# One scatter per expert into the output, and half of a plain float32 weight tile split in two

## The chip, the cores and the metric

One core of a Trainium2 chip runs the whole kernel. The metric is device microseconds for one execution, the median of several runs.

## The reference

A block of attention is followed by a mixture of experts, and the change lies in the second. The part that matters, cut:

```python
def hier_moe(u, wg, bg, we, be, w_gate, w_up, w_down):    # 2064 tokens, 64 experts in 8 groups
    g_p, g_idx = lax.top_k(g_prob, 1)                      # one group for each token
    e_p, e_idx = lax.top_k(jax.nn.softmax(e_logits, axis=-1), TOP_K)   # two experts of that group
    ...
    def expert_block(args):
        xb, e = args
        hdn = jax.nn.silu(xb @ w_gate[e]) * (xb @ w_up[e])   # 1024 -> 512
        return hdn @ w_down[e]                                # 512 -> 1024
    out = jnp.zeros((n_tok + 1, D), f32).at[slot_tok].add(ys.astype(f32) * slot_gate[:, None])[:n_tok]
...
    h = h + hier_moe(rmsnorm(h, ffn_norm[l]), ...)
return rmsnorm(h, final_norm)[:, N_META:]
```

Each token goes to two experts of one group. Its row of the result is the residual plus both experts' contributions, and then a norm over the row with the gains `final_norm`.

## The kernel before, in words

The kernel has an attention part (about the first 1200 us) and an expert part, `phase_moe`, which takes the rest. The expert part does one **turn** for each of the 64 experts, in an order that walks through the groups (the same group comes back every eight turns). An expert works on up to 112 token rows of 1024 numbers.

**Weights.** The three weight matrices of an expert come as six tiles of 128x2048 float32 numbers: g0 and g1 (gate), u0 and u1 (up), d0 and d1 (down). Five of them are split: ScalarE casts `raw` to a short float `hi`, VectorE subtracts, `lo = raw - hi`, and TensorE makes three cheap products in place of one (`mm3`: hi by hi, hi by lo, lo by hi). The sixth, d1, is multiplied as it is, in plain float32 (`down_whole`, rows `pd<-raw,hc`).

**A turn on TensorE**, always in this order: gate (M_g0, M_g1), turning the hidden rows of the expert before (TH), up (M_u0, M_u1), turning the next expert's rows (TX0, TX1), and down of the expert before (M_d0, M_d1a, M_d1).

**A turn on VectorE**, in the trace's names: `h` (the product with silu), `xl` twice (low parts of the token rows), `z` twice (the down result plus the row `b`), five `lo`, `o<-z,ss,gain` (the last norm), and `hl` (low parts of the hidden rows, without which M_d0 can't go past its second product).

**A turn on ScalarE**: five `hi`, `xh` twice, `sg` (silu), `o<-z` (squares, whose sum is `ss`), `hh` and `hc` (high parts and plain copy of the hidden rows).

**A turn on GpSimd**: `xs<-ud,src` gathers the token rows of a later expert; `b<-hz,src` gathers the rows of the array `hz` for the expert two turns on, into one of two buffers, so it has to wait for the second `z` of this turn; `hz<-z,t_zd` scatters `z` to `hz`; two small operations `ss` make the row's scale from the sum of squares (add EPS, power -0.5); `out_dram<-o,t_od` scatters the normed rows to the output. Both scatters are given all 112 rows. An index beyond 2047 makes a row be skipped: a token's first expert writes its row to `hz` alone, its second to the output alone (tables `t_zd` and `t_od`).

**Order.** `moe_plan` sets the order on TensorE, VectorE, ScalarE and GpSimd from a table of costs and due times, and `Ordered` keeps the compute instructions of an engine in it. Where the DMAs of GpSimd stand among them is settled when the program is built. Each engine works off its own queue in order: an instruction that waits holds up all behind it.

All expert instructions stand under the helper's line L124 in the profile (L123 after the change), so groups are told apart by their tiles.

Of the kernel before, what the change touches and what calls it, by code (L numbers as in the profile page):

```python
# [75 lines left out]
def build(tc, a, dbg=None, stop=99):  # L76
    nc = tc.nc
    dbg = dbg or {}
    with ExitStack() as top:
# [19 lines left out]
        nc.scalar.preload_act_table_set("natural_log_exp_and_others")  # L99
        env = dict(tc=tc, nc=nc, a=a, dbg=dbg, zf=zf, zv=zv, qd=qd, qrd=qrd, hg=hg, ud=ud, hz=hz, xlist=xlist, xexp=xexp,  # L100
                   ident=ident, ones=ones, eps=eps, out=a.get("out"))
        env["rt"] = {}
        with ExitStack() as ctx:
            env["ctx"] = ctx
            env["keep"] = ctx.enter_context(tc.tile_pool(name="keep", bufs=1))
            z_rest, z_close = phase_z(**env)
            env["right"] = right = ExitStack()
            kvp = right.enter_context(tc.tile_pool(name="kv", bufs=1, side=RIGHT))
            env["kv"] = ([kvp.tile([P, L], F32R, name=n) for n in ("ch", "cl", "kr_")]
                         + [kvp.tile([P, NT + 1, P], F32R, name=n) for n in ("vh", "vl")])  # L110
# [646 lines left out]

def phase_mix(tc, nc, a, qd, qrd, hg, ud, hz, xlist, xexp, kv, ident, ones, eps, rt, keep, ctx, right, g_rest, g_close, **_):
    ch, cl, kr_, vh, vl = kv
# [10 lines left out]
    with ExitStack() as out:  # L770
# [354 lines left out]
        def out_proj(i, xs, yh, yl, hs, t, hf):  # L1125
# [11 lines left out]
            if hf and hs[-1] == 3:  # L1137
                nc.sync.dma_start(hz[j * P:j * P + P], x)
# [277 lines left out]
def targets(nc, sp, rt):  # L1416
# [3 lines left out]
    first = first.rearrange("s g j -> s (g j)")  # L1420
    zd = rt["zd"] = sp.tile([BS, NE], I32, name="t_zd", bufs=1)
    od = rt["od"] = sp.tile([BS, NE], I32, name="t_od", bufs=1)
    nc.vector.scalar_tensor_tensor(od, first, float(FAR), rt["src"], op0=OP.mult, op1=OP.add)
    nc.vector.tensor_scalar(first, first, -float(FAR), float(FAR), op0=OP.mult, op1=OP.add)
    nc.vector.tensor_add(zd, first, rt["src"])


def moe_plan():
# [9 lines left out]
    for i, t in enumerate(TILES):  # L1438
        b, k = -(t[0] == "d"), i - HB
        old = ("M_" + TILES[k % n], -(k // n))  # L1440
        op("hi_" + t, b, "A", 1.95, old)
        op("lo_" + t, b, "V", 2.4, ("hi_" + t, 0), old)

# [3 lines left out]
    def cost(t):  # L1447
        return W if t in TILES else W * 4 / 3

# [92 lines left out]
    line.sort(key=lambda x: x[0])  # L1542
    return [(n, e, e + ops[n][0], nodes[n, e][0]) for _, (n, e) in line if n not in ("GD", "BQ", "ZQ", "OQ")]


def phase_moe(tc, nc, a, ctx, ud, hz, xlist, xexp, ident, ones, eps, rt, out, **_):
    rp = rt["rp"]
# [47 lines left out]
    def turn(S):  # L1595
        S.hn = 2 if NATIVE and S.e is not None else 4
        S.hh = sp.tile([P, 4, BS], F32R, name="hh", tag="hh", bufs=2)
# [11 lines left out]
    def hcopy(S):  # L1609
        S.hc = sp.tile([P, 2, BS], F32, name="hc", tag="hc", bufs=2)  # L1610
        on.scalar.copy(S.hc, S.ph[:, 2:])

    def down_whole(S, raw, hf):
        cs = slice(512 * hf, 512 * hf + 512)
        for k in range(2):
            on.tensor.matmul(S.d[hf], S.hc[:, k], raw[:, k, cs], start=False, stop=k == 1)

# [7 lines left out]
    rows = Block()  # L1625
    rows.put, rows.got, rows.sent = [], [], []

# [29 lines left out]

    def root(ss):
        on.gpsimd.tensor_scalar(ss, ss, EPS, None, op0=OP.add)
        on.gpsimd.tensor_tensor(ss, ss, half[:ss.shape[0]], op=OP.pow)  # L1660

    def last_norm(S):
        on.vector.scalar_tensor_tensor(S.o, S.z, S.ss, rows.gain[:BS], op0=OP.mult, op1=OP.mult)

    def leave(S):
        o = spread(out, rt["od"][:, S.e:S.e + 1], S.o)
        for q in rows.sent:
            tc.declare_no_dep(o.ins, q.ins, reason="rows of other tokens")
        rows.sent.append(o)

# [16 lines left out]
    def hi(S, t, eng):  # L1687
        load(S, t)
        if t == "d0" and NATIVE:
            load(S, "d1")  # L1690
        made[S.e, t].high(rp, eng)
# [7 lines left out]
    def mm_d(S, j, hf):  # L1699
        if f"d{j}" in NATIVE:  # L1700
            w = made[S.e, f"d{j}"] if hf == 0 else made.pop((S.e, f"d{j}"))
            return down_whole(S, w.view(w.raw), hf)
        w = made[S.e, f"d{j}"].parts() if hf == 0 else use(S, f"d{j}")
# [39 lines left out]
    with tc.For_i(0, again, 1):  # L1743
        nx = nc.values_load(nxi[0:1, 0:1], min_val=0, max_val=NX)
        with tc.For_i(0, nx, 1) as x:
# [34 lines left out]
            S.b = sp.tile([BS, D], F32, name="b", tag="b", bufs=BB)  # L1780
            gather(S.b, S.src, hz)
            for j in range(2):
# [16 lines left out]
            for hf in range(2):  # L1799
                plus(S, hf)  # L1800
            spread(hz, S.src, S.z)
        ft = sp.tile([P, NT, 8], F32, name="xft", tag="xft", bufs=1)
# [8 lines left out]
        for t in range(NT):  # L1811
            y = sp.tile([P, D], F32, name="xy", tag="z", bufs=ZB)
            nc.vector.memset(y, 0.0)
            gather(y, ix[:, t:t + 1], hz)
# [3 lines left out]
            root(ss)  # L1818
            nc.vector.scalar_tensor_tensor(o, y, ss, gain, op0=OP.mult, op1=OP.mult)
# [60 lines left out]
```

## Time and profile before

| what | value |
|---|---|
| median of 3 runs | 2450.58 us (2449.58 to 2459.94) |
| the profiled execution's own time | 2446.82 us |
| its span, first to last instruction | 2445.1 us |
| TensorE busy | 2350.4 us, 96% of the span |
| VectorE, ScalarE, GpSimd busy | 72%, 53%, 37% of the span |

The profiled execution took 1.72 us more than its span. Busy shares are averages over two parts with different limits; the expert part runs from about 1248 us to the end.

### The profile page before, as it was taken

The numbers are of one execution on the slowest core, as the hardware profiler recorded it, in microseconds if no ns is written. First come the engines' busy times: TensorE is split into PE (matmuls) and PEld (weight loads), VectorE is DVE, ScalarE is ACT, GpSimd is POOL, SyncE is SP. The second block draws the span as 40 slices with busy tenths as digits, with TensorE's granted clock in tenths as the row PEclk, the third lists the DMA queues.
The fourth block names the chain that finished last, engine by engine and source line by source line (L and its number), as shares of the span: only waits on it lengthen the run. The fifth ranks groups of instructions, "written<-read, shape, count | busy, mean of one in ns | idle before, by whom it ended". The sixth has DMA issues, their size and how long they took to land. (4 is left out here: it accounts for less than half of the span.)

```text
span 2445.1 us, 35600 instructions
## 1 busy us (share of the span) xinstructions
PE 2350.4 (96%) x12897; PEld 1870.6 (77%) x12897; DVE 1755.0 (72%) x2756; ACT 1303.9 (53%) x2018; POOL 905.4 (37%) x740
## 2 busy tenths in 40 slices
PE   7999999899999999999699999999999999999997
PEld 7899997677789989989566777676666666666664
DVE  6334334777567777767678888888888888888885
ACT  4211103555365555555366666666666666666663
POOL 0000002621000212111335556566656666666653
PEclk9999999899999999999899999999999999999999
DMA  6211115555331212111599999999999999999994
GB/s 210 76 62 66 65 43 158 167 164 178 130 109 61 79 61 82 55 68 44 218 326 389 380 386 376 386 375 381 369 367 367 375 370 381 369 366 375 374 359 182
DMA packets 161154, 571.70 MB, mean 234 GB/s; under 512 B 37132, under 2 KB 79644, under 8 KB 111820
## 3 DMA queue, kind: packets, MB, share of 16 engines
q1 hardware_dynamic: 125612, 509.71, 56.6%
q0 software_dynamic: 32912, 50.94, 6.5%
q10 hardware_dynamic: 2448, 8.72, 1.2%
q8 instruction: 103, 1.69, 0.3%
q14 instruction: 79, 0.65, 0.1%
HBM read 529.71 MB, written 106.63 MB: 260 GB/s over the span
## 5 line engine op out<-in xcount | busy, mean ns | idle before, releaser
L124 DVE TENSOR_TENSOR lo<-raw,hi 128x2048 fp32r<-128x2048 f32 x317 | 720.7, 2285 | 15.1 <-ACT hi L124 10.2
L124 ACT CAST hi<-raw 128x2048 fp32r<-128x2048 f32 x318 | 609.5, 1917 | 200.8 <-PE pg L124 132.7
L124 PE MATMUL pg<-hi,xh 128*112 128x512 f32 x1024 | 434.5, 424 | 0.0
L124 PE MATMUL pg<-hi,xl 128*112 128x512 f32 x1024 | 407.6, 398 | 2.7 <-DVE xl L124 2.7
L124 PE MATMUL pg<-lo,xh 128*112 128x512 f32 x1024 | 401.9, 392 | 0.0
L124 POOL DMA_INDIRECT hz<-z,t_zd x64 | 262.0, 4094 | 323.2 <-DVE z L124 314.5
L124 PEld LDWEIGHTS pg<-lo,xh 128*112 128x112 f32 x1024 | 180.5, 176 | 70.0 <-issue 7.1
L124 POOL DMA_INDIRECT out_dram<-o,t_od x64 | 193.6, 3025 | 105.0 <-DVE hl L124 82.4
L124 PEld LDWEIGHTS pg<-hi,xh 128*112 128x112 f32 x1024 | 179.3, 175 | 66.4 <-ACT xh L124 10.3
L124 PE MATMUL pd<-raw,hc 128*112 128x512 f32 x512 | 230.0, 592 | 0.0
L124 PEld LDWEIGHTS pg<-hi,xl 128*112 128x112 f32 x1024 | 178.9, 175 | 61.8 <-DVE xl L124 3.3
L135 PE MATMUL ps<-uh,wh 128*128 128x256 f32 (+3 forms) x768 | 218.7, 285 | 1.3 <-ACT uh L231 0.9
L136 PE MATMUL ps<-ul,wh 128*128 128x256 f32 (+3 forms) x768 | 218.3, 284 | 0.6 <-DVE ul L232 0.6
L137 PE MATMUL ps<-uh,wl 128*128 128x256 f32 (+3 forms) x768 | 217.4, 283 | 0.0
L124 DVE SCALAR_TENSOR_TENSOR o<-z,ss,gain 112x1024 f32<-112x1024 f32 x64 | 82.2, 1285 | 173.0 <-POOL ss L124 167.4
L124 PEld LDWEIGHTS pd<-raw,hc 128*112 128x112 f32 x512 | 90.1, 176 | 104.2 <-issue 97.0
L135 PEld LDWEIGHTS ps<-uh,wh 128*128 128x128 f32 (+1 forms) x768 | 144.7, 189 | 2.3 <-ACT uh L231 1.1
L136 PEld LDWEIGHTS ps<-ul,wh 128*128 128x128 f32 (+1 forms) x768 | 144.7, 188 | 1.5 <-DVE ul L232 0.8
L137 PEld LDWEIGHTS ps<-uh,wl 128*128 128x128 f32 (+1 forms) x768 | 144.7, 188 | 0.1
L124 POOL DMA_INDIRECT xs<-ud,src x64 | 126.6, 1978 | 40.7 <-issue 18.7
L338 POOL TENSOR_SCALAR_AFFINE_SELECT mf<-ones 128x128 f32<-128x128 f32 x2 | 0.6, 300 | 380.8 <-PE ps L137 380.8
L257 DVE COPY st<-ps 128x256 f32<-128x256 f32 (+1 forms) x64 | 26.9, 422 | 143.6 <-PE ps L137 143.6
(2413 smaller groups left out, 5302.8 us busy)
## 6 DMA issues: line engine op xcount, KB each, us to landing
raw<-in_w_gate_dram SPq DMA_DIRECT2D x128, 1024.0 KB
raw<-in_w_up_dram SPq DMA_DIRECT2D x128, 1024.0 KB
raw<-in_w_down_dram SPq DMA_DIRECT2D x128, 1024.0 KB
x<-in_x_dram SPq DMA_DIRECT2D x32, 512.0 KB
zf<-st SPq DMA_DIRECT2D x85, 128.0 KB
hg<-x SPq DMA_DIRECT2D x16, 512.0 KB
x<-hg SPq DMA_DIRECT2D x16, 512.0 KB
hz<-x SPq DMA_DIRECT2D x16, 512.0 KB
```

The costliest lines, as they stand in the source:

```text
L124: return self.tc.keep_in_program_order(f(*args, **kw))
L135: nc.tensor.matmul(out, lh, rh, start=start, stop=False, **kw)
L136: nc.tensor.matmul(out, lh, rl, start=False, stop=False, **kw)
L137: nc.tensor.matmul(out, ll, rh, start=False, stop=stop, **kw)
L257: nc.vector.tensor_copy(st[:w, :n - o], ps[:w, :n - o])
L338: nc.gpsimd.affine_select(mf[:, :, hh], ob, pattern=[[CH, 2], [1, CH]], compare_op=OP.is_ge, fill=0.0, base=0, channel_multiplier=-1)
```

## The change

1. The array `hz` goes. The residual is written to the output array itself, the rows `b` are gathered from there, and each expert scatters once, to the output: `out_dram<-o,src`, with all its tokens' rows.
2. What a row needs is chosen by numbers in place of indices. For a token's first expert the exponent of `ss` is 0 (table `t_hx`) and the gains are 1; for its second they are -0.5 and `final_norm`. ScalarE forms the matrix of gains for each expert (`GM`, an operation over 112x1024 numbers, `g<-gain,t_first,t_sec`), and the last norm reads `g` where it read `gain`.
3. Of the tile d1, the first 1024 of 2048 columns are split in hi and lo and multiplied by `mm3`; the other 1024 stay plain float32. So there is a sixth `hi` and a sixth `lo` in a turn, both of half width; `hl` and `hh` take 336 columns in place of 224, `hc` 112 in place of 224.
4. The planner's table follows: the scatter to `hz` (SZ) is out, GM is in, due times are moved.

```diff
-NATIVE = ("d1",)
-TILES = tuple(t for t in ("g0", "g1", "u0", "u1", "d0", "d1") if t not in NATIVE)
+TILES = ("g0", "g1", "u0", "u1", "d0", "d1")
+SPLIT = 1
...
-            eng.copy(self.hi, self.raw)
+            eng.copy(self.hi[:, :self.n], self.raw[:, :self.n])
...
-            eng.tensor_sub(self.lo, self.raw, self.hi.bitcast(F32))
+            eng.tensor_sub(self.lo[:, :self.n], self.raw[:, :self.n], self.hi[:, :self.n].bitcast(F32))
...
-    od = rt["od"] = sp.tile([BS, NE], I32, name="t_od", bufs=1)
-    nc.vector.scalar_tensor_tensor(od, first, float(FAR), rt["src"], op0=OP.mult, op1=OP.add)
...
+    sec = rt["sec"] = sp.tile([BS, NE], F32, name="t_sec", bufs=1)
+    nc.vector.tensor_scalar(sec, first, -1.0, 1.0, op0=OP.mult, op1=OP.add)
+    rt["fst"] = first
+    hx = rt["hx"] = sp.tile([BS, NE], F32, name="t_hx", bufs=1)
+    nc.vector.tensor_scalar_mul(hx, sec, -0.5)
...
-    op("GB", -1, "G", 1.7, ("Y1", BB), ("ZQ", 8))
+    op("GB", -1, "G", 1.7, ("Y1", BB), ("OQ", 8))
     op("BQ", -1, "Q", 5.0, ("GB", 0))
-    op("SZ", -1, "G", 2.1, ("Y1", 0))
-    op("ZQ", -1, "Q", 5.0, ("SZ", 0))
     op("SQ", -1, "A", 1.3, ("Y1", 0), ("OQ", OB))
-    op("RT", -1, "G", 0.3, ("SQ", 0))
-    op("L", -1, "V", 1.3, ("RT", 0))
+    op("RT", -1, "G", 1.3, ("SQ", 0))
+    op("GM", -1, "A", 1.1, ("L", 2))
+    op("L", -1, "V", 1.3, ("RT", 0), ("GM", 0))
...
-        for n, d in (("SZ", 2.5), ("SQ", 6.0), ("L", 9.0), ("SO", 10.0)):
+        for n, d in (("SQ", 3.0), ("L", 7.0), ("SO", 8.5)):
...
+        for k in range(SPLIT):
+            mm3(on, S.d[hf], S.hh[:, 2 + k], S.hl[:, 2 + k], hi[:, k, cs], lo[:, k, cs], False, False)
+        for k in range(SPLIT, 2):
+            on.tensor.matmul(S.d[hf], S.hc[:, k - SPLIT], raw[:, k, cs], start=False, stop=k == 1)
...
-        o = gather(S.b, S.src, hz)
+        o = gather(S.b, S.src, out)
...
+    def blend(S):
+        S.g = sp.tile([BS, D], F32, name="g", tag="g", bufs=2)
+        on.scalar.activation(S.g, rows.gain[:BS], AF.Identity, scale=rt["sec"][:, S.e:S.e + 1], bias=rt["fst"][:, S.e:S.e + 1])
...
-        on.vector.scalar_tensor_tensor(S.o, S.z, S.ss, rows.gain[:BS], op0=OP.mult, op1=OP.mult)
+        on.vector.scalar_tensor_tensor(S.o, S.z, S.ss, S.g, op0=OP.mult, op1=OP.mult)
...
-        o = spread(out, rt["od"][:, S.e:S.e + 1], S.o)
+        o = spread(out, S.src, S.o)
```

GpSimd, a turn in the middle of the expert part before the change, from one scatter to the output to the two `ss` operations, all turns alike:

```order
L124 DMA out_dram<-o,t_od 2048x1024
L124 DMA xs_13720<-ud,src 112x1024
L124 DMA hz<-z,t_zd 2048x1024
L124 DMA b<-hz,src 112x1024
L124 TENSOR_SCALAR ss<-ss 112x1
L124 TENSOR_TENSOR ss<-ss,half 112x1
```

GpSimd with the change, such a turn in the form that most have:

```order
L123 DMA out_dram<-o,src 2048x1024
L123 DMA b<-out_dram,src 112x1024
L123 DMA xs_13719<-ud,src 112x1024
L123 TENSOR_SCALAR ss<-ss 112x1
L123 TENSOR_TENSOR ss<-ss,t_hx 112x1
```

The scatter to `hz` is gone, and the gather `xs`, which stood ahead of it, now stands between the gather `b` and the two `ss`. That is so in 42 of the 64 turns (in two of these between the two `ss`); in the others `xs` stands ahead of `b` or behind the `ss`, so that `b` alone stands there, and in the last two neither does.

VectorE, the end of a turn and the start of the next before the change, around the last norm `o`:

```order
L124 TENSOR_TENSOR z<-pd,b 112x512
L124 TENSOR_TENSOR lo_19832<-raw,hi 128x2048
L124 TENSOR_TENSOR lo_19847<-raw,hi 128x2048
L124 SCALAR_TENSOR_TENSOR o<-z,ss,gain 112x1024
L124 TENSOR_TENSOR hl<-pth,hh 128x224
L124 TENSOR_TENSOR lo_19739<-raw,hi 128x2048
L124 TENSOR_TENSOR lo_19773<-raw,hi 128x2048
```

VectorE with the change, the same place:

```order
L123 TENSOR_TENSOR z<-pd,b 112x512
L123 TENSOR_TENSOR lo_19960<-raw,hi 128x2048
L123 TENSOR_TENSOR lo_19974<-raw,hi 128x2048
L123 SCALAR_TENSOR_TENSOR o<-z,ss,g 112x1024
L123 TENSOR_TENSOR hl<-pth,hh 128x336
L123 TENSOR_TENSOR lo_20015<-raw,hi 128x1024
L123 TENSOR_TENSOR lo_20033<-raw,hi 128x2048
L123 SCALAR_TENSOR_TENSOR h<-pg,grs,sg 112x128x4
L123 TENSOR_TENSOR xl<-pt,xh 128x448
L123 TENSOR_TENSOR lo_20055<-raw,hi 128x2048
```

The last norm still stands behind two `lo` of full width, and `hl` right behind the norm. The half-width `lo` of d1 is new, `hl` is wider, and one of the two `lo` that stood ahead of `h` has moved behind `xl`.

## Rows read from the trace of the kernel before

**Rows 1.** The page's first part: busy time, share, instructions by engine.

```profile
PE 2350.4 (96%) x12897; PEld 1870.6 (77%) x12897; DVE 1755.0 (72%) x2756; ACT 1303.9 (53%) x2018; POOL 905.4 (37%) x740
```

**Rows 2.** Busy time by stretch: stretch, length, busy (instructions) by engine, clock, DMA share, GB/s.

```profile
1230.00:1240.00 10.00, 8.74 (x33) 6.47 (x34) 7.27 (x14) 3.37 (x4) 0.58 (x1) 0.83 1.02 369
...
2100.00:2200.00 100.00, 99.06 (x424) 68.81 (x423) 84.12 (x64) 64.96 (x64) 61.12 (x31) 1.00 0.98 368
```

**Rows 3.** Timeline of TensorE, starts of plain products of d1: start, length, what.

```profile
1248.37 3.59 PE L124 MATMUL pd<-raw,hc 128*112 128x512 f32 x8
...
1619.90 3.59 PE L124 MATMUL pd<-raw,hc 128*112 128x512 f32 x8
...
1675.90 3.59 PE L124 MATMUL pd<-raw,hc 128*112 128x512 f32 x8
...
2400.54 3.59 PE L124 MATMUL pd<-raw,hc 128*112 128x512 f32 x8
```

**Rows 4.** Timeline of TensorE: plain and split products, and a wait in brackets.

```profile
1452.72 3.59 PE L124 MATMUL pd<-raw,hc 128*112 128x512 f32 x8
...
1456.39 0.39 PE L124 MATMUL pg<-lo,xh 128*112 128x512 f32 x1
...
1461.48 0.39 PE L124 MATMUL pg<-hi,xl 128*112 128x512 f32 x1
...
2054.84 0.49 PE L124 MATMUL pd<-hi,hl 128*112 128x512 f32 x1 [0.19 <-DVE hl L124]
```

**Rows 5.** Timeline, a turn of 19.07 us: VectorE, GpSimd and ScalarE around the last norm.

```profile
1641.85 0.61 DVE L124 TENSOR_TENSOR xl<-pt,xh 128x448 fp32r<-128x448 f32 x1
1642.38 2.28 DVE L124 TENSOR_TENSOR lo<-raw,hi 128x2048 fp32r<-128x2048 f32 x1
1644.58 0.68 DVE L124 TENSOR_TENSOR z<-pd,b 112x512 f32<-112x512 f32 x1
1645.18 4.48 DVE L124 TENSOR_TENSOR lo<-raw,hi 128x2048 fp32r<-128x2048 f32 x2
1645.54 4.96 POOL L124 DMA_INDIRECT hz<-z,t_zd  x1 [4.77 <-DVE z L124]
1646.81 1.05 ACT L124 ACTIVATE o<-z 112x1024 f32<-112x1024 f32 x1
1650.81 0.99 POOL L124 DMA_INDIRECT b<-hz,src  x1 [0.30 <-issue]
1652.80 1.29 DVE L124 SCALAR_TENSOR_TENSOR o<-z,ss,gain 112x1024 f32<-112x1024 f32 x1 [3.14 <-POOL ss L124]
1654.01 0.38 DVE L124 TENSOR_TENSOR hl<-pth,hh 128x224 fp32r<-128x224 f32 x1
1654.31 4.60 DVE L124 TENSOR_TENSOR lo<-raw,hi 128x2048 fp32r<-128x2048 f32 x2
```

**Rows 6.** Timeline, a turn of 18.58 us: VectorE and GpSimd ahead of the last norm.

```profile
1570.40 2.76 POOL L124 DMA_INDIRECT hz<-z,t_zd  x1 [5.27 <-DVE z L124]
1572.53 2.29 DVE L124 TENSOR_TENSOR lo<-raw,hi 128x2048 fp32r<-128x2048 f32 x1 [0.21 <-ACT hi L124]
1573.46 2.23 POOL L124 DMA_INDIRECT b<-hz,src  x1 [0.30 <-issue]
1576.70 1.28 DVE L124 SCALAR_TENSOR_TENSOR o<-z,ss,gain 112x1024 f32<-112x1024 f32 x1 [1.87 <-POOL ss L124]
```

**Rows 7.** Groups by line from 1660 to 2380 us: count, busy, mean ns, idle before.

```profile
L124 DVE SCALAR_TENSOR_TENSOR o<-z,ss,gain 112x1024 f32<-112x1024 f32 x38 | 48.8, 1285 | 119.7 <-POOL ss L124 119.7
...
L124 POOL DMA_INDIRECT hz<-z,t_zd x38 | 188.8, 4968 | 183.5 <-DVE z L124 183.5
```

**Rows 8.** Timeline of GpSimd near the end, where VectorE stands still.

```profile
2425.53 0.95 POOL L124 DMA_INDIRECT hz<-z,t_zd  x1 [5.21 <-DVE z L124]
```

**Rows 9.** Waits from 1300 to 2300 us: who waited for whom, total, times, longest.

```profile
ACT hc L124 <- DVE hl L124: 163.5, 52, 4.9
...
ACT hi L124 <- PE pg L124: 104.7, 49, 3.7
```

More of the change, by code (lines that the diff above doesn't have):

```diff
@@ L1440, in moe_plan @@
         old = ("M_" + TILES[k % n], -(k // n))
-        op("hi_" + t, b, "A", 1.95, old)
-        op("lo_" + t, b, "V", 2.4, ("hi_" + t, 0), old)
+        op("hi_" + t, b, "A", 1.05 if t == "d1" else 1.95, old)
+        op("lo_" + t, b, "V", 1.2 if t == "d1" else 2.4, ("hi_" + t, 0), old)
     def ready(t):
@@ L1447, in cost @@
     def cost(t):
-        return W if t in TILES else W * 4 / 3
+        return W * 7 / 6 if t == "d1" else W
     for i, t in enumerate(("g0", "g1", "u0", "u1")):
@@ L1542, in moe_plan, with phase_moe @@
     line.sort(key=lambda x: x[0])
-    return [(n, e, e + ops[n][0], nodes[n, e][0]) for _, (n, e) in line if n not in ("GD", "BQ", "ZQ", "OQ")]
-def phase_moe(tc, nc, a, ctx, ud, hz, xlist, xexp, ident, ones, eps, rt, out, **_):
+    return [(n, e, e + ops[n][0], nodes[n, e][0]) for _, (n, e) in line if n not in ("GD", "BQ", "OQ")]
+def phase_moe(tc, nc, a, ctx, ud, xlist, xexp, ident, ones, eps, rt, out, **_):
     rp = rt["rp"]
@@ L1595, in turn @@
     def turn(S):
-        S.hn = 2 if NATIVE and S.e is not None else 4
+        S.hn = 2 + SPLIT if S.e is not None else 4
         S.hh = sp.tile([P, 4, BS], F32R, name="hh", tag="hh", bufs=2)
@@ L1609, in hcopy, with down_whole @@
     def hcopy(S):
-        S.hc = sp.tile([P, 2, BS], F32, name="hc", tag="hc", bufs=2)
-        on.scalar.copy(S.hc, S.ph[:, 2:])
-    def down_whole(S, raw, hf):
+        S.hc = sp.tile([P, 2 - SPLIT, BS], F32, name="hc", tag="hc", bufs=2)
+        on.scalar.copy(S.hc, S.ph[:, 2 + SPLIT:])
+    def down_whole(S, w, hf):
         cs = slice(512 * hf, 512 * hf + 512)
-        for k in range(2):
-            on.tensor.matmul(S.d[hf], S.hc[:, k], raw[:, k, cs], start=False, stop=k == 1)
+        hi, lo = w.parts()
+        raw = w.view(w.raw)
+        for k in range(SPLIT):
+            mm3(on, S.d[hf], S.hh[:, 2 + k], S.hl[:, 2 + k], hi[:, k, cs], lo[:, k, cs], False, False)
+        for k in range(SPLIT, 2):
+            on.tensor.matmul(S.d[hf], S.hc[:, k - SPLIT], raw[:, k, cs], start=False, stop=k == 1)
     def down(S, j, w, hf):
@@ L1625, in phase_moe @@
     rows = Block()
-    rows.put, rows.got, rows.sent = [], [], []
+    rows.put, rows.got = [], []
     def apart(o, S, old):
@@ L1656, in phase_moe, with root @@
     nc.vector.memset(half, -0.5)
-    def root(ss):
+    def root(ss, half):
         on.gpsimd.tensor_scalar(ss, ss, EPS, None, op0=OP.add)
-        on.gpsimd.tensor_tensor(ss, ss, half[:ss.shape[0]], op=OP.pow)
+        on.gpsimd.tensor_tensor(ss, ss, half, op=OP.pow)
+    def blend(S):
+        S.g = sp.tile([BS, D], F32, name="g", tag="g", bufs=2)
+        on.scalar.activation(S.g, rows.gain[:BS], AF.Identity, scale=rt["sec"][:, S.e:S.e + 1], bias=rt["fst"][:, S.e:S.e + 1])
     def last_norm(S):
-        on.vector.scalar_tensor_tensor(S.o, S.z, S.ss, rows.gain[:BS], op0=OP.mult, op1=OP.mult)
+        on.vector.scalar_tensor_tensor(S.o, S.z, S.ss, S.g, op0=OP.mult, op1=OP.mult)
     def leave(S):
-        o = spread(out, rt["od"][:, S.e:S.e + 1], S.o)
-        for q in rows.sent:
-            tc.declare_no_dep(o.ins, q.ins, reason="rows of other tokens")
-        rows.sent.append(o)
+        o = spread(out, S.src, S.o)
+        apart(o, S, rows.put + rows.got)
+        rows.put.append((o, S.e // 8))
     def block(xs, g, u, d, grs, rs, src, e=None, i=None):
@@ L1688, in hi @@
         load(S, t)
-        if t == "d0" and NATIVE:
-            load(S, "d1")
+        if t == "d1":
+            made[S.e, t].n = 1024 * SPLIT
         made[S.e, t].high(rp, eng)
@@ L1699, in mm_d @@
     def mm_d(S, j, hf):
-        if f"d{j}" in NATIVE:
-            w = made[S.e, f"d{j}"] if hf == 0 else made.pop((S.e, f"d{j}"))
-            return down_whole(S, w.view(w.raw), hf)
+        if j:
+            return down_whole(S, made[S.e, "d1"] if hf == 0 else made.pop((S.e, "d1")), hf)
         w = made[S.e, f"d{j}"].parts() if hf == 0 else use(S, f"d{j}")
@@ L1780, in phase_moe @@
             S.b = sp.tile([BS, D], F32, name="b", tag="b", bufs=BB)
-            gather(S.b, S.src, hz)
+            gather(S.b, S.src, out)
             for j in range(2):
@@ L1800, in phase_moe @@
                 plus(S, hf)
-            spread(hz, S.src, S.z)
+            spread(out, S.src, S.z)
         ft = sp.tile([P, NT, 8], F32, name="xft", tag="xft", bufs=1)
@@ L1813, in phase_moe @@
             nc.vector.memset(y, 0.0)
-            gather(y, ix[:, t:t + 1], hz)
+            gather(y, ix[:, t:t + 1], out)
             ss = sp.tile([P, 1], F32, name="xss", tag="xss", bufs=1)
@@ L1817, in phase_moe @@
             nc.scalar.activation(o, y, AF.Square, scale=D ** -0.5, accum_out=ss)
-            root(ss)
+            root(ss, half)
             nc.vector.scalar_tensor_tensor(o, y, ss, gain, op0=OP.mult, op1=OP.mult)
```

30 lines of the change are left out of this document (11 added, 19 removed).

## The prediction, made before the result was known

> **What bounds the kernel now.** The page's first part shows TensorE busy for 96% of the span [rows 1], which looks like the bound. The busy times by stretch agree in the expert part: 99.06 of 100 us late in it, at full granted clock, with VectorE at 84.12 [rows 2]. A busy share doesn't tell who waits for whom, though, so the next view is the timeline of TensorE, and in it one event per turn: the start of the plain products of d1. There are 62 such starts from 1248.37 to 2400.54 us, so 61 turns take 1152.2 us [rows 3], and they fall in two kinds. The first 20 take (1619.90 - 1248.37) / 20 = 18.58 us each. Three turns of transition lie up to 1675.90. The last 38 take (2400.54 - 1675.90) / 38 = 19.07 us each.
>
> In the short turns TensorE is the bound, and its work fills the turn. In the long ones it waits in each turn for `hl` from VectorE [rows 4]; TensorE is late there because VectorE is. The reader is to see why in the timeline of a long turn [rows 5]. The second `z` releases the scatter to `hz` on GpSimd, which starts at 1645.54, just after two chained `lo` have begun on VectorE. The `lo` end at 1645.18 + 4.48 = 1649.66 and the scatter at 1650.50, 0.84 us later, after 4.96 us. With VectorE idle near the end the same scatter takes 0.95 us [rows 8]. So GpSimd gets nowhere with a DMA while the `lo` run, and needs some 0.85 us after them. Then come the gather `b` (0.30 us of issue, 0.99 us, to 1651.80) and the two `ss` (1.00 us), while VectorE stands with the last norm `o` at the head of its queue, and `hl` and all later `lo` behind it: 3.14 us from the end of the `lo` to 1652.80. All 38 long turns show it: scatters of 4.97 us and 119.7 / 38 = 3.15 us of waiting for `ss` [rows 7].
>
> In a short turn there is a gap of 0.21 us between the two `lo`, because a `hi` is late; the scatter slips in and is done in 2.76 us. Only the gather `b` is then held until the second `lo` ends at 1574.82; it ends 0.87 us after that, and `o` follows at 1576.70, with 1.87 us of waiting [rows 6].
>
> So a long turn is a loop on VectorE: 19.07 us, of which 3.14 are waiting for GpSimd and 15.93 are work, small waits included. A turn lasts as long as the longer of that loop and TensorE's work.
>
> **The change, step by step.** *TensorE.* A plain product of 512 columns has two records; eight records take from 1452.72 to 1456.16 (one step ahead of 1456.39), 0.43 us each, so 0.86 us a product [rows 4]. Split products follow each other at (1461.48 - 1456.39) / 22 = 0.231 us [rows 4]. Two plain products become six split ones: 1.72 - 1.39 = 0.33 us less. TensorE alone would need 18.58 - 0.33 = 18.24 us for a turn.
>
> *VectorE.* A full `lo` holds the engine for 2.20 us when work follows (1642.38 to 1644.58) [rows 5]. The new one of 1024 columns is not in the trace. Half of 2.20 is 1.10 from below; `o`, also 1024 columns, takes 1.21 to the start of `hl` [rows 5] and bounds it from above. I take 1.13, nearer to the same operation. `hl` takes 0.30 us at 224 columns, `xl` 0.53 at 448 [rows 5]; at 336 that is 0.42, so 0.12 more. A wait of about 0.09 us inside the pair of `lo` behind `hl` (4.60 against 4.48 us [rows 5]) goes, since the pair is now a half and a full one, whose `hi` is ready. Work becomes 15.93 + 1.13 + 0.12 - 0.09 = 17.09 us.
>
> *GpSimd.* The scatter to `hz` goes, but `b` is released by the same second `z` and now takes its place: it starts under the two `lo`, is held, and ends about 0.85 us after them. What follows depends on the order. Where `xs` stands behind `b`, ahead of or between the two `ss` (42 turns), it issues for 0.30 us and runs for 0.95 to 1.03 us, like any such DMA with VectorE idle (0.95 in [rows 8], 0.99 in [rows 5]; I take 0.99), and then the `ss` take 1.00 us. That is the old 3.14 us again. Where `b` alone stands there, it is 0.87 + 1.00 = 1.87 us, as in the short turns [rows 6]. The output scatter waits for `o` as before; it and a gather behind it have the rest of the turn.
>
> So the loop is 17.09 + 3.14 = 20.23 us in 42 turns and 17.09 + 1.87 = 18.96 us in the others. Both exceed TensorE's 18.24. The gap that let the scatter slip in before can't last: it comes from a `hi` that waits for TensorE, and with VectorE 0.7 us or more longer per turn than TensorE, VectorE is late within some three turns and finds that `hi` done. Those first turns (0 to 2, which have `b` alone) I put at 18.24 us.
>
> *ScalarE* gains GM (1.05 us like the squares, the same 112x1024 [rows 5]) and a half `hi` (about 1.0, half of a full cast). It idles 163.5 / 52 = 3.1 us a turn ahead of `hc` and 104.7 / 49 = 2.1 us ahead of a `hi` [rows 9], so about 2 us are hidden; were that cover gone, they would delay a `lo` and so add to the loop. GM is computed a turn ahead, so `o` doesn't wait for it. *DMA:* every scatter skipped the rows that the other wrote, so the bytes stay alike; their one new dependency (`b` behind the output scatter of eight turns ago) is long met. The first 1248 us and the tail after the last counted turn I leave as they are: in the tail 0.3 us less per product of d1 stands against the new `lo`.
>
> **The sum.** 42 x 20.23 + 16 x 18.96 + 3 x 18.24 = 849.7 + 303.4 + 54.7 = 1207.8 us for 61 turns, against 1152.2: 55.6 us more. The profiled execution took 2446.82, so about 2502; the median of the runs shown is 3.8 us above it, so **2506**. With 1.10 or 1.21 for the new `lo`, and 0.95 or 1.03 for `xs`, this moves by 58 x 0.08 = 4.6 and 42 x 0.04 = 1.7 us up or 3.4 down; with an uncertain start, its own range is 2492 to 2518.
>
> One rule speaks against this. The rows say that a DMA on GpSimd is held across both chained `lo` (4.96 us, to 0.84 after the second [rows 5]). The Trainium skill, SBUF — State Buffer, section "Who interferes with whom", says that a VectorE instruction with two SBUF inputs contends with a GpSimd instruction that reads SBUF, and that the first to issue keeps the shared ports for its whole instruction. If the hold ended with each instruction, `b` would come through after the first `lo`, and the result would be that of the second rival below; the long turns' rows disagree, so the sum goes by the rows.
>
> **The rivals.** *TensorE stays the bound (faster).* If the `ss` came within 18.24 - 17.09 = 1.15 us of the last `lo`, all turns would take 18.24: 1112.6 us, 39.6 less, **2411**. For it: a scatter of up to 4.96 us is removed just ahead of the `ss`, and the `ss` alone take 1.00. Against it: `b` is released at the same point and has no gap to slip into; both DMAs would have to be through beforehand. From 0.3 us above that point on, a turn is no faster than the short ones of before.
>
> *`b` gets through early (no change).* If it passed after the first `lo`, only `xs` would be held, and the `ss` would follow after 1.87 us in every turn: 58 x 18.96 + 54.7 = 1154.4, 2 us more, **2453**. The short turns show how little it takes, a gap of 0.21 us; against it stand 38 long turns in a row without one.
>
> *The clock falls too (slower still).* TensorE would pause 20.23 - 18.24 = 2.0 us a turn, a tenth. In 1230 to 1240 us, with 1.3 of 10 us idle, the granted clock was 0.83, a mixture of its two levels, 1.2 and 2.4 GHz [rows 2]. At 0.83 its work takes 22.0 us, 1.7 more than the loop: 42 x 1.7 = 71 more, **2577**. Against it: pauses of a few tenths in each long turn left it at 1.00 [rows 2].
>
> **How the numbers follow.** Chances: my forecast 0.70, `b` early 0.13, TensorE the bound 0.10, the clock 0.05; 0.02 for something else that is slower. A change under 0.5% (12 us) can't be told from none here: three runs span 10 us. So slower 0.77, same 0.13, faster 0.10. The range goes from 2447, to take in `b` early, to 2525, which leaves out the fastest and the slowest case and holds 0.83.
>
> **What would show it.** Starts of the plain products 20.2 us apart in most turns and 19.0 in some; `b` at 4.9 us, ending 0.85 us behind two chained `lo`; `xs` behind it at about 1 us; `o` waiting 3.1 or 1.9 us for `ss`; TensorE waiting for `hl` for 1 to 2 us. The forecast is wrong if `b` ends under the `lo` pair, or the pair has a gap, or `lo` at half width costs other than 1.1 us.

## The result: 8% slower, by a wait that the prediction left out

| | before | with the change |
|---|---|---|
| median (4 runs of each, side by side) | 2454.83 us | 2660.06 us (2656.38 to 2660.89) |
| ratio, 95% interval | | 1.0833 (1.0802 to 1.0865) |
| profiled execution: own time, span | 2446.82, 2445.1 us | 2656.38, 2654.4 us |

The prediction was 2506 us, 2447 to 2525. The sign was right; the loss is 205 us instead of 55.

The page's first part, to be read beside [rows 1]: busy time, share of the span, instructions.

```profile
PE 2405.4 (91%) x13025; PEld 1942.2 (73%) x13025; DVE 1827.9 (69%) x2819; ACT 1449.5 (55%) x2146; POOL 697.3 (26%) x676
```

VectorE has gained 73 us of work and lost share; ScalarE has gained 146 us and two points of share; neither is near full. TensorE is busy for 55 us *more*, though its work shrank, and for less of the span. The waits of the 1200 us from 1300 to 2500 tell who waits (engine, instruction, what it waited for: us in total, times, longest):

```profile
POOL b L123 <- DVE z L123: 492.5, 54, 10.4
DVE o L123 <- POOL ss L123: 280.7, 54, 8.7
...
POOL xs L123 <- PE pt L123: 168.1, 50, 6.9
PEld pd L123 <- DVE hl L123: 157.4, 40, 5.7
...
PE pd L123 <- DVE hl L123: 139.7, 39, 5.2
```

The first is idle time of an engine that is early. The other four belong together: `o` waits for `ss`, TensorE waits for `hl`, which stands behind `o`, and, new, the gather `xs` waits for TensorE (`pt`, the turning of the token rows). The timeline shows how, in one turn of each kind (start, length, engine, what, and the idle time before it with what ended it):

```profile
1336.64 4.48 DVE L123 TENSOR_TENSOR lo<-raw,hi 128x2048 fp32r<-128x2048 f32 x2
1336.99 5.06 POOL L123 DMA_INDIRECT b<-out_dram,src  x1 [10.32 <-DVE z L123]
1342.12 0.23 POOL L123 TENSOR_SCALAR ss<-ss 112x1 f32<-112x1 f32 x1
1343.05 1.28 DVE L123 SCALAR_TENSOR_TENSOR o<-z,ss,g 112x1024 f32<-112x1024 f32 x1 [1.93 <-POOL ss L123]
...
1378.55 4.48 DVE L123 TENSOR_TENSOR lo<-raw,hi 128x2048 fp32r<-128x2048 f32 x2
1378.90 5.06 POOL L123 DMA_INDIRECT b<-out_dram,src  x1 [10.34 <-DVE z L123]
1386.21 1.04 PE L123 MATMUL pt<-ident,xs 112*128 112x112 f32 x8
1387.52 0.99 POOL L123 DMA_INDIRECT xs<-ud,src  x1 [3.56 <-PE pt L123]
1388.58 0.24 POOL L123 TENSOR_SCALAR ss<-ss 112x1 f32<-112x1 f32 x1
1388.90 0.58 POOL L123 TENSOR_TENSOR ss<-ss,t_hx 112x1 f32<-112x1 f32 x1
1389.51 1.28 DVE L123 SCALAR_TENSOR_TENSOR o<-z,ss,g 112x1024 f32<-112x1024 f32 x1 [6.47 <-POOL ss L123]
1390.71 0.50 DVE L123 TENSOR_TENSOR hl<-pth,hh 128x336 fp32r<-128x336 f32 x1
1391.27 0.65 PE L123 MATMUL pd<-hi,hl 128*112 128x512 f32 x1 [3.56 <-DVE hl L123]
```

The upper turn, `b` alone ahead of the `ss`, is what was forecast: `b` ends 0.93 us behind the `lo` pair, `o` waits 1.93 us. In the lower one `b` ends at 1383.96, likewise, but then `xs` doesn't issue. It stands idle for 3.56 us until TensorE has turned the token rows (1386.21 to 1387.25), then takes 0.99 us as priced; the `ss` and `o` follow. There are three buffers for token rows. In the queue with the `ss` of expert i stands `xs` of expert i+6, whose buffer is that of i+3, and TensorE turns the rows of i+3 at the end of the turn, right ahead of M_d0 of expert i+1. That M_d0 needs `hl` of i+1, and `hl` stands behind `o` of i. So the loop no longer runs over two engines but over three, and nearly all of TensorE's turn is in it: M_d0, M_d1, gate, up, TX, then `xs`, `ss`, `o`, `hl`, and M_d0 again. Nearly every time round, TensorE stands still for 3.56 us.

From the second to the 60th `o` (1282.82 to 2570.47) there are 58 turns of 22.20 us in the mean. 16 take 18.8 to 19.0 us, 10 take 22.7 to 22.9, 18 take 23.5 to 23.7 and 9 take 24.3 to 25.8; five, of 19.5 to 22.4, are mixed. The steps go with the granted clock, as the busy time of TensorE by stretch shows for three single turns with the same 82 products (stretch, length, busy with instructions, clock, DMA share, GB/s):

```profile
1582.59:1604.71 22.12, 18.56 (x82) 1.00 0.82 298
1831.97:1855.63 23.66, 20.10 (x82) 0.93 0.81 297
1855.63:1880.05 24.42, 20.87 (x82) 0.86 0.76 275
```

Where the clock was 0.93 or 0.86, a mixture of 1.2 and 2.4 GHz, TensorE's work takes 1.54 or 2.31 us longer, and so does the turn, because TensorE is inside the loop. The turns of 22.9 us are of another kind: each follows a short one, has no pause and a clock of 1.00, and works off what that one left over (99 products). Before the change, in the row of 2100 to 2200 us [rows 2], the clock was 1.00.

A second loss lies in the tail. From the 60th `o` to the last (2377.42 to 2433.69 before, 2570.47 to 2639.37 after) it takes 68.9 us in place of 56.3. ScalarE and VectorE there, in the timeline of the changed kernel:

```profile
2574.95 1.91 ACT L123 CAST hi<-raw 128x2048 fp32r<-128x2048 f32 x1 [1.77 <-PE pd L123]
...
2599.11 1.90 ACT L123 CAST hi<-raw 128x2048 fp32r<-128x2048 f32 x1 [6.94 <-PE pd L123]
2601.04 2.29 DVE L123 TENSOR_TENSOR lo<-raw,hi 128x2048 fp32r<-128x2048 f32 x1 [5.50 <-ACT hi L123]
```

A `hi` waits 6.94 us for a product that frees one of the four `hi` buffers, and a `lo` behind it 5.50. In the plan the last expert's `hi` of d0 and d1 have no gate tile of a later expert to wait for and are put two turns early; in the last turns they break the order in which the buffers go round.

### The profile page after: what moved, and what is told of

Read it like the earlier page. It is cut to its first block, busy times and chain, and to the rows that moved or that the text cites. A ratio compares the mean times of both kernels' runs of the same rounds, so it can differ in the third digit from the quotient of the medians.

```text
span 2654.4 us, 36048 instructions
## 1 busy us (share of the span) xinstructions
PE 2405.4 (91%) x13025; PEld 1942.2 (73%) x13025; DVE 1827.9 (69%) x2819; ACT 1449.5 (55%) x2146; POOL 697.3 (26%) x676
## 2 busy tenths in 40 slices
DMA packets 152964, 571.69 MB, mean 215 GB/s; under 512 B 28940, under 2 KB 71452, under 8 KB 103628
## 5 line engine op out<-in xcount | busy, mean ns | idle before, releaser
L123 ACT CAST hi<-raw 128x2048 fp32r<-128x2048 f32 x382 | 673.6, 1764 | 413.7 <-PE pd L123 189.7
L123 DVE TENSOR_TENSOR lo<-raw,hi 128x1024 fp32r<-128x1024 f32 (+1 forms) x381 | 791.0, 2099 | 23.7 <-ACT hi L123 23.5
L123 POOL DMA_INDIRECT b<-out_dram,src x64 | 294.9, 4607 | 574.9 <-DVE z L123 574.5
L123 PE MATMUL pd<-hi,hl 128*112 128x512 f32 x384 | 186.6, 486 | 150.0 <-DVE hl L123 150.0
L123 DVE SCALAR_TENSOR_TENSOR o<-z,ss,g 112x1024 f32<-112x1024 f32 x64 | 82.2, 1284 | 306.4 <-POOL ss L123 306.4
L123 PEld LDWEIGHTS pd<-hi,hl 128*112 128x112 f32 x384 | 83.3, 217 | 196.5 <-DVE hl L123 169.7
L123 PE MATMUL pd<-hi,hh 128*112 128x512 f32 x384 | 208.4, 543 | 4.1 <-ACT hh L123 4.1
L123 PE MATMUL pd<-lo,hh 128*112 128x512 f32 x384 | 178.6, 465 | 0.0
L123 POOL DMA_INDIRECT xs<-ud,src x64 | 100.5, 1570 | 210.4 <-PE pt L123 197.1
L123 PE MATMUL pd<-raw,hc 128*112 128x512 f32 x256 | 131.8, 597 | 0.0
```

The costliest lines, as they stand in the source:

```text
L123: return self.tc.keep_in_program_order(f(*args, **kw))
```

## The experiments

All ratios are against the kernel before, run on the same chip at the same time. The first four ran beside a median of 2459.65 us, e5 to e8 beside 2458.91, e9 to e11 beside 2461.71, and the changed kernel beside 2454.83; so a difference between medians of different groups is good to some 7 us.

| run | median us | ratio, 95% interval | mean turn, 2nd to 60th `o` |
|---|---|---|---|
| e1 `xs` behind the `ss` | 2467.67 | 1.0043 (1.0025 to 1.0060) | 18.95 |
| e2 one scatter, d1 plain | 2434.56 | 0.9901 (0.9865 to 0.9937) | 18.54 |
| e3 split only | 2541.65 | 1.0341 (1.0304 to 1.0379) | 20.21 |
| e4 `xs` and `b` behind the `ss` | 2443.32 | 0.9940 (0.9920 to 0.9960) | 18.45 |
| e5 `xs` between, buffer free | 2547.21 | 1.0359 (1.0342 to 1.0376) | 20.22 |
| e6 e1 with a memset in the pair | 2447.94 | 0.9958 (0.9944 to 0.9972) | 18.51 |
| e7 e4 with the tail in order | 2426.78 | 0.9861 (0.9839 to 0.9882) | 18.52 |
| e8 before, DMAs behind the `ss` | 2588.21 | 1.0516 (1.0497 to 1.0535) | 21.17 |
| e9 e7 without the load of u1 | 2414.99 | 0.9818 (0.9788 to 0.9848) | 18.27 |
| e10 the change, last `hi` of d0 in order | 2648.16 | 1.0759 (1.0724 to 1.0794) | 22.21 |
| e11 before with a memset in the pair | 2433.57 | 0.9896 (0.9866 to 0.9926) | 18.63 |

The theory after the trace (A): `xs`, queued ahead of the `ss`, waits for TensorE to free its buffer. Its rivals: the lower clock is the cause and not a result (B); the added work on VectorE and ScalarE, `hi` above all, is the cause (C).

**e1, `xs` out of the way.** The gather is queued behind the second `ss` of the turn (`rows.root`); all else is the changed kernel.

```diff
+    def fetch(S):
+        if rows.root is None:
+            return gather(S.xs, S.src, ud)
+        with tc.issue_after(rows.root.ins):
+            gather(S.xs, S.src, ud)
...
-    do = {"GA": lambda S, g: gather(S.xs, S.src, ud),
+    do = {"GA": lambda S, g: fetch(S),
```

> The changed kernel with one edit: the gather xs on GpSimd is queued behind the two ss operations in every turn. Theory A (the long turns of 23.6 us come from xs, which waits for TensorE to free its buffer and holds the ss, the last norm and hl behind it, so that TensorE waits for itself): no turn with xs ahead of ss is left, every turn is of the kind that now takes 18.95 to 19.0 us, the wait of the last norm is 1.9 us, and the time is 61 x (19.0 - mean of before 18.89) = 7 us above before, so 2455 to 2465. Theory B (the granted clock, which fell from 0.986 to 0.953, makes the turns long): TensorE still pauses 0.7 us a turn, the clock stays under 0.96 and the time above 2550. Theory C (the added work on VectorE and ScalarE and waits for hi make them long): little changes, above 2600.

Of the 205 us of loss, 8 are left, with nothing changed but one gather's place in a queue (the time lies 3 us above the expected range). Nearly every turn is like the short ones of the changed kernel, in the timeline of e1:

```profile
1861.21 4.49 DVE L123 TENSOR_TENSOR lo<-raw,hi 128x2048 fp32r<-128x2048 f32 x2
1861.57 5.00 POOL L123 DMA_INDIRECT b<-out_dram,src  x1 [7.05 <-DVE z L123]
...
1867.58 1.28 DVE L123 SCALAR_TENSOR_TENSOR o<-z,ss,g 112x1024 f32<-112x1024 f32 x1 [1.88 <-POOL ss L123]
```

The clock is 1.00 from 1300 to 2350 us, all added work is still there, and so is the longer tail (70.4 us). B and C fall as main causes: without the wait the clock doesn't drop.

**e2 and e3, the two halves of the change alone.** e2 has one scatter and GM, with d1 plain; e3 is the kernel before with half of d1 split, by the lines of points 3 and 4 of the change. The core of e2, against the changed kernel:

```diff
-TILES = ("g0", "g1", "u0", "u1", "d0", "d1")
-SPLIT = 1
+TILES = ("g0", "g1", "u0", "u1", "d0")
+SPLIT = 0
```

> Only the first half of the change: one scatter per expert and the gains formed on ScalarE, while d1 stays wholly plain float32. On GpSimd xs stands ahead of b here, and b alone between the second z and the ss. Theory A: VectorE's loop is 15.9 + 1.9 = 17.8 us, under TensorE's 18.58, so TensorE bounds all turns as in the first 20 of before: 61 x (18.58 - 18.89) = -19 us, 2430 to 2440, the clock at 1.00 in the expert part. Theory B: the same, since TensorE doesn't pause. Theory C: GM adds 1 us on ScalarE and no VectorE work, so 2430 to 2480.

> Only the second half of the change: half of d1 split in hi and lo, with the array hz and both scatters as before. The scatter to hz and the gather b stand between the second z and the ss, xs does not. Theory A: VectorE's loop is 17.1 + 3.14 = 20.2 us in nearly all turns, so 58 x 20.2 + 3 x 18.2 against 1152 is 75 us more: 2520 to 2535, with no wait for TensorE on GpSimd ahead of the ss; TensorE pauses 2 us a turn. Theory B: those pauses lower the clock and the time is well above that, 2580 or more. Theory C: as slow as the whole change, 2600 to 2660.

One scatter alone gains 1.0%: TensorE, with 18.57 us of work, is busy for all of 1300 to 2350 us. VectorE is early here, so a `hi` is late and leaves a gap in the pair of `lo`, through which `b` passes; so it goes in 54 of 58 turns, as the second rival had it.

```profile
1835.48 2.28 DVE L123 TENSOR_TENSOR lo<-raw,hi 128x2048 fp32r<-128x2048 f32 x1
1835.84 2.79 POOL L123 DMA_INDIRECT b<-out_dram,src  x1 [5.90 <-DVE z L123]
1838.51 2.29 DVE L123 TENSOR_TENSOR lo<-raw,hi 128x2048 fp32r<-128x2048 f32 x1 [0.74 <-ACT hi L123]
1841.59 1.28 DVE L123 SCALAR_TENSOR_TENSOR o<-z,ss,g 112x1024 f32<-112x1024 f32 x1 [0.79 <-POOL ss L123]
```

The split alone loses 3.4%, 7 us more than the top of the expected range (its tail, 65.2 us against 56.3, accounts for 9). Its timeline shows a loop of the forecast's length: three chained `lo`, the scatter to `hz` held under them, `b`, the `ss`, and 3.14 us of waiting.

```profile
1845.75 6.69 DVE L125 TENSOR_TENSOR lo<-raw,hi 128x2048 fp32r<-128x2048 f32 x3
1846.12 7.14 POOL L125 DMA_INDIRECT hz<-z,t_zd  x1 [4.86 <-DVE z L125]
1853.56 1.00 POOL L125 DMA_INDIRECT b<-hz,src  x1 [0.30 <-issue]
...
1855.58 1.28 DVE L125 SCALAR_TENSOR_TENSOR o<-z,ss,gain 112x1024 f32<-112x1024 f32 x1 [3.14 <-POOL ss L125]
```

The halves add up to 25 us less and 82 us more, 57 in sum. That this comes near the 55 forecast for the whole is chance: the gap that helps e2 is gone once the split makes VectorE late, and `xs` stands ahead of the `ss` in neither. The whole costs 205, since the wait for the buffer belongs to neither half but to the order that came of both.

**e4, both gathers behind the `ss`.** As e1, with `b` there too; in the planner's table, too, `b` now waits for the `ss`.

```diff
-          "GB": lambda S, g: base(S),
+          "GB": lambda S, g: behind(base, S),
```

> The changed kernel with both gathers, b and xs, queued behind the two ss operations, so that nothing stands between the second z and the ss on GpSimd. Theory A: the last norm waits only for the two ss, 1.0 to 1.2 us behind the last lo, VectorE's loop is 18.1 to 18.3 us, and TensorE's own 18.24 bounds the turn: 61 x (18.25 - 18.89) = -39 us, 2410 to 2425, clock 1.00 in the expert part. Theory B: the same if TensorE doesn't pause. Theory C: the added VectorE and ScalarE work still holds TensorE up: above 2450.

2443 us: faster than before, but 18 us or more short of what was expected. `o` waits 0.79 us in the best turns, as it should. Two things were missed. The tail is one (e7). The other is in the waits from 1300 to 2350 us of e4:

```profile
ACT hi L123 <- DMA raw<-in_w_down_dram: 126.9, 80, 3.6
```

**e5, the wait alone.** The decisive one. `xs` stays where it hurts, between `b` and the `ss`, now in 58 turns instead of 42, right behind `b`, but has a fourth buffer, and so one that TensorE left a turn ago.

```diff
-XSB = 3
+XSB = 4
...
+    def fetch(S):
+        if S.i - 4 not in rows.base:
+            return gather(S.xs, S.src, ud)
+        with tc.issue_after(rows.base[S.i - 4].ins):
+            gather(S.xs, S.src, ud)
```

> The changed kernel with four buffers for the gathered token rows in place of three, and the gather xs held at its place: behind b and ahead of both ss, now in 58 turns. Its buffer was read for the last time a whole turn earlier, so it has nothing to wait for. Buffer theory (xs waits for TensorE's turning of the token rows): xs issues at once when b is done, o waits 3.1 us for ss, turns of 20.2 us throughout, 58 x 20.22 + 3 x 18.24 = 1227 for the 61 turns, about 75 more than before and 12 in the tail: 2530 to 2545 us. Rival (xs behind b costs its time whatever its buffer, because the queue or the DMA engines are busy): o still waits 5.8 us or more for ss and the turns stay at 22.9 to 24.4 us: 2660 us or more, since xs stands there in more turns.

113 us less than the changed kernel, though `xs` stands there 16 times more. In its timeline `xs` issues at once:

```profile
1843.95 5.04 POOL L123 DMA_INDIRECT b<-out_dram,src  x1 [10.31 <-DVE z L123]
1849.29 0.98 POOL L123 DMA_INDIRECT xs<-ud,src  x1 [0.30 <-issue]
...
1851.28 1.28 DVE L123 SCALAR_TENSOR_TENSOR o<-z,ss,g 112x1024 f32<-112x1024 f32 x1 [3.21 <-POOL ss L123]
```

The turns take 20.28 us; the forecast loop was 20.23. So the step's prices held, and what it lacked was the wait for the buffer. (The time lies 2 us above what was expected.)

**e6, the hold.** e1 with a memset of one column on VectorE between the two chained `lo`.

```diff
+    gap = sp.tile([BS, 1], F32, name="gap", bufs=1)
...
     def lo(S, t, eng):
+        if t == "d0":
+            on.vector.memset(gap, 0.0)
```

> The kernel with xs behind both ss (turns of 18.96 us, o waits 1.88 us), with one tiny memset on VectorE between the two chained lo. Theory of the hold (a DMA on GpSimd gets nowhere while lo follows lo, and slips in at a gap between them): b is done at about 0.9 us after the first lo or in the gap, the squares and the ss follow sooner, o waits 0.8 to 1.2 us, turns of 18.25 us (TensorE is the bound): about 2467 - 60 x 0.7 = 2425 us. Rival (the hold goes on over any VectorE instruction that follows without an idle time, or b is late for another reason): 18.96 us a turn, 2467 us as without the memset, or a few us more.

```profile
1725.19 4.49 DVE L123 TENSOR_TENSOR lo<-raw,hi 128x2048 fp32r<-128x2048 f32 x2
1725.54 2.82 POOL L123 DMA_INDIRECT b<-out_dram,src  x1 [7.04 <-DVE z L123]
1727.42 0.06 DVE L123 MEMSET gap<- 112x1 f32 x1
...
1730.47 1.28 DVE L123 SCALAR_TENSOR_TENSOR o<-z,ss,g 112x1024 f32<-112x1024 f32 x1 [0.79 <-POOL ss L123]
```

In this timeline `b` ends at 1728.36, while the second `lo` still runs; without the memset it took 5.00 us. An instruction of 0.06 us lets the DMA in, in nearly every turn: `b` takes 2.8 us in the turns without idle time between the two `lo`, as in this one, too. The gain, 20 us, is half of what was expected: here too `hi` waits for `raw`, as in e4.

**e7, e10, the tail.** In the plan, `hi` of d0 is held behind `hi` of d1 of the expert before, and `hi` of d1 behind that of d0 of its own expert; ahead of the last turns this moves a cast in one turn alone. e7 is e4 with both holds, by these lines. e10 is the changed kernel with the first hold alone, so the last `hi` of d1 still stands two turns early there.

```diff
-        op("hi_" + t, b, "A", 1.05 if t == "d1" else 1.95, old)
+        last = {"d0": [("hi_d1", 1)], "d1": [("hi_d0", 0)]}.get(t, [])
+        op("hi_" + t, b, "A", 1.05 if t == "d1" else 1.95, old, *last)
```

> Both gathers behind the ss (as in the kernel that took 2443 us), and in the plan the two casts of the last expert's down tiles are held behind those of the expert before, so that the order of ScalarE and the ring of hi buffers in the last turns is that of all others. Theory of the tail (early casts of the last expert take two of the four hi buffers and stop ScalarE, then VectorE, for 22.2 and 27.8 us in place of twice 18.6 or so in the last two full turns): intervals of o near the end of 18.3 to 19.5 us, 10 to 14 us less: 2429 to 2433 us. Rival (the long last turns come from something else, such as late raw tiles): 2440 us or more with the intervals still above 22 and 26 us.

> The changed kernel with nothing but the casts of the last expert's down tiles held back in the plan; xs stays between b and the ss in 42 turns. Buffer theory: the turns stay at 18.95 to 19.0, 22.9, 23.65 and 24.4 us, since the cause of the loss lies there, and only the last turns shorten: 2660 less 12 to 17 us, 2643 to 2648 us. Rival (the early casts disturb more than the tail, or the plan's order elsewhere moves the turns): outside 2635 to 2655 us.

e7 has the lowest time of the versions with no work left out, 1.4% under the kernel before (its interval overlaps that of e11). Its last four intervals of `o` take 53.1 us (17.86 for the last of a full turn); in e4 they were 72.4. In e10 they take 58.0 in place of 68.9, the time falls by 12 us, and the wait for the buffer, from 1300 to 2500 us, is untouched:

```profile
POOL xs L123 <- PE pt L123: 169.6, 50, 6.9
```

**e8, the same order for the kernel before.** Scatter to `hz`, `b` and `xs` behind the `ss`.

```diff
-    op("SZ", -1, "G", 2.1, ("Y1", 0))
+    op("SZ", -1, "G", 2.1, ("Y1", 0), ("RT", 0))
...
-    do = {"GA": lambda S, g: gather(S.xs, S.src, ud),
+    do = {"GA": lambda S, g: behind(gather, S.xs, S.src, ud),
...
-          "GB": lambda S, g: base(S), "SZ": lambda S, g: keep_z(S),
+          "GB": lambda S, g: behind(base, S), "SZ": lambda S, g: behind(keep_z, S),
```

> The kernel before, unchanged but for the order on GpSimd: scatter to hz, b and xs all stand behind the two ss. Theory (the 3.14 us of waiting in its long turns is the hold on the scatter plus what stands ahead of the ss): o waits under 1.2 us, all turns 18.57 us where TensorE is the bound: 38 x (19.07 - 18.57) = 19 us less, 2430 to 2441 us. Rival (the hold only moves: b then comes late for z, or the scatter delays it): z waits for b, turns of 19 us or more, 2450 us or more.

The rival came true. `o` waits only 0.79 us, but `b`, queued behind the scatter, is now fetched for the very next expert, and `z` waits for it, in the waits from 1300 to 2540 us and in a turn of the timeline:

```profile
DVE z L124 <- DMA b<-hz,src: 253.2, 58, 6.8
```

```profile
1793.16 2.17 POOL L124 DMA_INDIRECT b<-hz,src  x1 [0.30 <-issue]
...
1802.87 0.69 DVE L124 TENSOR_TENSOR z<-pd,b 112x512 f32<-112x512 f32 x1 [4.64 <-DMA b<-hz,src]
```

With one scatter (e4) `b` stays two experts ahead in this order; with two it didn't. Whether another order of the three DMAs would keep it ahead wasn't tried.

**e9, the next bound.** e7, where u1 has no load of its own.

```diff
-            made[S.e, t] = Weight(nc, rp, *S.w[t[0], int(t[1])])
+            made[S.e, t] = Weight(nc, rp, *S.w[t[0], int(t[1])], made[S.e, "u0"].raw if t == "u1" else None)
```

> The kernel that took 2427 us (both gathers behind the ss, the last casts held back), but the tile u1 is not loaded: its hi and lo are made from the tile u0, so that part of the experts' result is computed with the wrong weights. The work of the engines stays, the DMA bytes fall by one of six tiles a turn. Theory of the DMA wall (at 384 GB/s and a busy share of 1.01 the raw tiles come late, and hold turns at 18.5 us in the mean): no hi waits for raw, the DMA share falls to about 0.87, all turns take TensorE's 18.24 us: 60 x 0.27 = 16 us less, about 2410 us. Rival (the turns above 18.24 come from something else, such as the order on ScalarE): the turns stay at 18.5 us in the mean, 2427 us.

The stretch from 1300 to 2350 us, of e7 and then of e9 (busy PE, PEld, DVE, ACT, POOL; clock, DMA share, GB/s):

```profile
1300.00:2350.00 1050.00, 1041.97 (x4664) 764.14 (x4663) 969.07 (x737) 828.85 (x798) 412.34 (x285) 1.00 1.01 384
```

```profile
1300.00:2350.00 1050.00, 1050.00 (x4723) 774.90 (x4722) 982.52 (x749) 842.93 (x811) 415.01 (x290) 1.00 0.93 330
```

With a sixth of the weights not moved, no `hi` waits for `raw`, and nearly all turns take 18.2 to 18.3 us: TensorE's own time, as forecast (18.24). With all weights, e7 stays at 18.52, with a DMA share of 1.01. So the loads bound it. Whether by bytes or by buffers isn't shown: in e9 the six `raw` buffers also serve five tiles a turn in place of six.

**e11, the hold in the kernel before.** The memset of e6 in the kernel before, with the same two lines.

> The kernel before with one memset of one column on VectorE between the two chained lo that stand ahead of the last norm. Theory of the hold (the scatter to hz slips in at the gap, as it does by itself in the short turns): the scatter takes 2.8 us in place of 4.97, b is then held by the second lo alone, o waits 1.9 us in place of 3.15, all turns 18.58 us: 38 x 0.49 = 19 us less, about 2436 to 2441 us. Rival (the short turns are short because a hi is late, and the gap itself does nothing): long turns of 19.07 us, 2455 us.

From 1660 to 2380 us the scatters to `hz` take 2.72 us each, where they took 4.97 [rows 7]; `o` waits 1.87 us in place of 3.15:

```profile
L124 POOL DMA_INDIRECT hz<-z,t_zd x39 | 106.2, 2724 | 223.0 <-DVE z L124 213.8 <-issue 9.2
```

The long turns are gone: 18.63 us in the mean, and the time is 1.0% less. This is the reading of [rows 5, 6], tried by itself. In 52 of the 58 turns from 1300 to 2380 us the pair then has a gap of its own as well, since VectorE is no longer late; in the six without one the scatter takes 2.76 to 2.78 us, too.

## Why the prediction was wrong, point by point

*The step that failed* stands under GpSimd: where `xs` stands behind `b`, "it issues for 0.30 us and runs for 0.95 to 1.03 us, like any such DMA with VectorE idle". The run time was right (0.99), the release was left out. It was priced like a DMA that has only its queue to wait for. In the trace of before that is what its rows say; the tile view of `xs` there, from 1300 to 2400 us, gives all its idle time as issue:

```profile
L124 POOL DMA_INDIRECT xs<-ud,src x56: 2002/2029/2722, 1303.0 to 2344.2; - x56
its engine sat idle before it (us, times) until:
  issue: 17.2, 56
```

But there `xs` stood behind the scatter of `o`, and `o` is later than the turning of the rows. The change put it ahead of the `ss`, on which `o` waits; from there the buffer isn't free yet. The order showed the move, and the prediction counted its time in the new place without asking what releases it there.

*What it cost.* By the forecast's own prices 58 turns take 42 x 20.23 + 16 x 18.96 = 1153.0 us; they took 1287.65. The difference is 134.6 us. An estimate of its parts, from the turns: at a clock of 1.00 the loop takes 22.1 us (two turns show it), and 42 x (22.1 - 20.23) = 79 is the wait itself; the lower clock adds 18 x 1.54 + 8 x 2.3 = 46; the rest, some 10, lies in turns that work off what a turn at a lower clock left over. e5 gives the same total by another way: 2547 us with 58 turns of 20.28; with 42 of them and 16 of 19.0 it would be 16 x 1.3 = 21 us less, 2526, and the changed kernel took 134 more.

*The tail*, left as it is in the prediction, cost some 12 us (68.9 against 56.3 in the traces; e10, with one cast put back, is 12 us faster), because early casts of the last expert change the order on ScalarE. With both, 2660 - 134 - 12 = 2514, against 2506.

*What held.* TensorE's 18.24 us (18.2 to 18.3 in e9). The loop with `b` alone, 18.96 us (18.8 to 19.0 in after, 18.95 in e1). The old 3.14 us with a DMA behind the held one (3.14 in e3, 3.21 in e5) and 20.23 us for it (20.2, 20.28). Half a `lo`, 1.13 us: a half and a full one take 3.42 us in the rows of e1 and a full one 2.28 to 2.29, which leaves 1.13. (The wait in the pair behind `hl`, put at 0.09, is 0.12 by its two rows in [rows 5]: 2 us in the sum.) The DMA bytes: 571.70 MB before, 571.69 after. GM and the sixth `hi` hidden: e1, with both in it, has turns of 18.95. That `b` is held through the whole pair was right (5.06 us, to 0.93 behind the second `lo`), against the rule by instruction.

*The rivals.* "TensorE stays the bound" and "`b` gets through early" both asked for the `ss` to come sooner; e4 and e6 had to make that by hand, and in e2, without the split, the second came about by itself. "The clock falls too" was nearest in time (2577). The clock did fall, from 1.00 to 0.94 over 1300 to 2350 us, but behind pauses of 3.56 us that it hadn't foreseen. In the loop that it assumed it didn't come true: in e5, with pauses of 1.4 us a turn (1050 less 979.4 us of busy TensorE, in 52 turns), the clock was 0.98 and the turns stayed at 20.28, since VectorE sets them.

## What to carry to other kernels

When a transfer moves in a queue, price its wait before its work: ask who reads its buffer last, and whether that reader itself waits, over however many engines, for something behind the transfer in the queue. A trace in which it never waited tells only of the place where it stood. And a small operation on which a whole engine waits shouldn't stand behind a prefetch: here the place of two gathers and the order of a few casts in the tail decided between 8% lost and 1.4% gained, for the same work on the engines.

## What the runs showed of the hardware

**A hold goes on from instruction to instruction, and a very small one ends it.** A DMA on GpSimd that starts under chained `lo` took 5.0 us with two (e1) and 7.14 with three (e3), ending 0.82 to 0.93 us behind the last in e3, e1 and the changed kernel; with a memset of 0.06 us between the two it took 2.82 us (e6, in a turn where VectorE shows no idle time) and 2.72 in the mean (e11). The Trainium skill, SBUF — State Buffer, section "Who interferes with whom", has a VectorE instruction with two SBUF inputs contend with GpSimd's reads for as long as that instruction runs. The runs agree that such instructions block (0.95 us in [rows 8], 4.96 in [rows 5]); that the hold goes on when another such instruction follows at once, and ends with a memset between, is what they add. Whether the memset lets the DMA in because it has no input or because it parts the two wasn't tried.

**The DMA engines gave 384 GB/s** over 1050 us at a busy share of 1.01 (e7), where `hi` waits 154 us for the `raw` tiles of down; with a sixth less loaded no `hi` waits for one (e9). The Trainium skill, SBUF — State Buffer, section "Summary: rules for kernel authors", gives about 358 GB/s for moves between HBM and SBUF; the figure here is 7% higher, and it is the one to reckon with in this kernel.

**The clock follows pauses of TensorE.** From 1300 to 2350 us it was 1.00 in e1 (the longest wait for `hl` 0.9 us), 0.98 in e5 (pauses of 1.4 us a turn) and 0.94 in the changed kernel (pauses of 3.56 us; 0.82 to 1.00 by turn).
